# Twelve of each block's 32 scale and shift steps of a norm on VectorE in place of ScalarE

## The chip, the cores and the metric

The kernel runs on one core of one Trainium2 chip. The metric is the device time of one execution in microseconds. The weights lie in HBM; the two token blocks' activations stay in the core's memory from the first layer to the last.

## The reference

Two layers of a decoder over 256 tokens of width 2048. Each layer has a mixer and a SwiGLU FFN, each behind an RMS norm whose result is scaled and shifted per channel by vectors that are computed from a conditioning vector `c`:

```python
def rms_norm(x, gain):
    xf = x.astype(jnp.float32)
    y = xf * lax.rsqrt(jnp.mean(xf * xf, axis=-1, keepdims=True) + EPS)
    return (y * gain.astype(jnp.float32)).astype(x.dtype)
...
# a layer, in words:
#   shift1, scale1, gate1, shift2, scale2, gate2 = silu(c) @ w_mod + b_mod
#   x += gate1 * mixer(rms_norm(x) * (1 + scale1) + shift1) @ w_out
#   x += gate2 * (silu(h @ w_gate) * (h @ w_up)) @ w_down,  h = rms_norm(x) * (1 + scale2) + shift2
```

The mixer is one input projection `w_in`, whose columns go to gated linear attention (GLA), sliding-window attention and a gated DeltaNet, and one output projection `w_out`. Behind the last layer stands one more norm with `final_gain`, without scale and shift steps.

## The kernel before

The 256 tokens are two blocks of 128 (`NB`), the 2048 channels 16 tiles of 128 (`KD`). All large products go through `stream`: a weight's row of 128 channels comes by DMA into `raw` (L321, on SP's queue), ScalarE rounds it to `wh` (L328), VectorE makes the rest `wl = raw - wh` (L329), and TensorE multiplies both blocks' activations, themselves split in two parts `hm`, with them (L356). Rows that are taken whole (`k in whole`) skip L328 and L329; so does all of layer 0's `w_out`.

`norm(l, sub, blk, r, res)` makes the activations of one block; `sub` is 0 for the mixer's norm and 1 for the FFN's. It goes by groups `j` of four channel tiles. VectorE scales the block's 512 columns by the inverse root mean square `r` (L450), TensorE transposes the four tiles into one PSUM bank `ps` (L453; tag `ga` or `mm`, three banks in all), ScalarE applies scale and shift to each tile, from PSUM into the tile `h32` (L456, four steps), ScalarE rounds all four to `hm` (L459), and VectorE makes the rest (L460). Scale and shift are per-partition columns `mod_col`, since the channels are the partitions here. A block has four groups, so 16 steps, and a norm of both blocks 32. There are four norms between products: layer 0's mixer norm at the start, layer 0's FFN norm (566 to 585 us in the profile), layer 1's mixer norm (1365 to 1388) and layer 1's FFN norm (1817 to 1836).

The modulation vectors of later norms are computed in the background: `mod_segment` loads rows of `w_mod` into `mraw` (L218, SP) and VectorE multiplies and adds them into `acc` (L221, one 128x1024 instruction for a row). `rate` sets how many of these steps stand beside a weight row. In an FFN norm `held` puts a small column of the last group's `hm` into `hold`: the next `mraw` is first written by GpSimd from it (L216), so its load waits for the norm. Behind layer 1's FFN norm SP also loads `final_gain`, 1 MB, into `fg` (L1136).

At the end of the mixer the last group of input columns (264 + 264, for GLA) is evicted by ScalarE in pieces (L975), partly with SiLU, while the attention's softmax takes exponentials on ScalarE (L913, L916; its rows are `b`, `neg`, `tot`). SiLU and exponential need different function tables; an `ACT_TABLE_LOAD` stands where the set changes.

The order of the work is not that of the source. The framework's scheduler puts the instructions of each engine into one list by its own estimate of when each can start, and every engine works its list strictly in order; waits are put in where an operand comes from another engine, or a buffer or a PSUM bank is still in use there.

Of the kernel before, what the change touches and what calls it, by code (L numbers as in the profile page):

```python
# [15 lines left out]
AF = mybir.ActivationFunctionType  # L16
ALU = mybir.AluOpType
AX = mybir.AxisListType

P = 128  # L20
# [83 lines left out]
def trunk(ctx: ExitStack, tc, x, cT, pos, small, consts, b_mod, w_mod, w_in, w_gk, w_out,  # L104
# [22 lines left out]
    def tl(pool, shape, tag, dt=F32, bufs=None):  # L127
        return pool.tile(shape, dt, tag=tag, name=nm(tag), bufs=bufs)
# [5 lines left out]
    def bank(tag="mm"):  # L134
        if tag == "any":
            which[0] += 1
            tag = "ga" if which[0] % 3 == 0 else "mm"
        return tl(psm, [P, 512], tag, bufs=1 if tag == "ga" else 2)

    V, A, G, TE, SY = nc.vector, nc.scalar, nc.gpsimd, nc.tensor, nc.sync  # L140
# [55 lines left out]
    mod_col, gate_row = {}, {}  # L196
# [85 lines left out]
    def need(table, key):  # L282
        while key not in table:
            if fins:
                fins.popleft()[1]()
            else:
                mods.popleft()[1]()
        return table[key]
# [147 lines left out]
    def norm(l, sub, blk, r, res, ks=range(KD)):  # L436

        at = ks[0]
        while at <= ks[-1]:
            j, i0 = divmod(at, 4)  # L440
            n = min(4 - i0, ks[-1] + 1 - at)
            if j not in res:
                res[j] = (tl_h32(), *(tl(hmp, [P, 4, P], "hm", F32R) for _ in range(2)))
            h32, hh, hl = (t[:, i0:i0 + n] for t in res[j])
            xn = scr[0]()[:, :n * P]
            x_j = xs[:, blk, at * P:(at + n) * P]
            if XN_ACT[l][sub]:
                A.activation(xn, x_j, AF.Copy, scale=r)
            else:
                V.tensor_scalar(xn, x_j, r, None, ALU.mult)  # L450
            ps = bank("any")
            for i in range(n):
                TE.transpose(ps[:, i * P:(i + 1) * P], xn[:, i * P:(i + 1) * P], ident)  # L453
            for i in range(n):
                need(mod_col, (l, 3 * sub + 1, at + i))
                A.activation(h32[:, i], ps[:, i * P:(i + 1) * P], AF.Identity,  # L456
                             scale=mod_col[l, 3 * sub + 1, at + i],
                             bias=mod_col[l, 3 * sub, at + i])
            A.activation(hh, h32, AF.Copy)  # L459
            V.tensor_tensor(hl, h32, hh.bitcast(F32), ALU.subtract)  # L460
            at += n
        return res

    def tl_h32():
        return scr[0]().rearrange("p (a b) -> p a b", a=4)
# [491 lines left out]
    def layer(l):  # L957
# [94 lines left out]
        for bi, ks in enumerate(blocks):  # L1052
            first, last = bi == 0, bi == len(blocks) - 1
            rate[1] = RATE_LAST if last and l == 0 else RATE_IN[l]
            if last:
                closed.difference_update({(l, GATE1), (l, SHIFT2), (l, SCALE2)})
            for blk in range(NB):
                norm(l, 0, blk, rms[blk], h[blk], ks)
            for name in ("qk", "z", "v"):
                project(name)  # L1060
            if l == 0 and first:
                for o in range(0, n_mask, 512):
                    n = min(512, n_mask - o)
                    t = scr[1]()
                    SY.dma_start(t[:, :n], consts[:, N_FULL + o:N_FULL + o + n])
                    V.tensor_copy(masks[:, o:o + n], t[:, :n])
            if last:
                mix.clear()
                for blk in range(NB):
                    for group in (3, 1, 2):  # L1070
                        mix[blk, group] = tl(hmp, [P, 4, P], "hm")
                        G.memset(mix[blk, group][:, 0, 0:1], 0.0)
                    for name in ("gqk", "gv", "gz"):
                        G.memset(slot(hmp, "hm", (name, blk))[:, 0:1], 0.0)
                kT = swa_keys(pb, both("kv"))
                gdn(l, pg, [dict(enumerate(both(n))) for n in "qkv"], both("z"), both("cbca"))
            project("bq")
# [31 lines left out]
        def after_w_out(blk, j, ps, half, final):  # L1109
            add_gated(l, GATE1, blk, half * 2 + j, ps, final)  # L1110
            if final and half == 1 and j == 1:
                rms[blk] = inv_rms(blk)
                h[blk] = held(blk, norm(l, 1, blk, rms[blk], {}))
# [112 lines left out]
```

## Time and profile before

| | us |
|---|---|
| three runs | 2586.03, 2591.96, 2594.05 |
| their median | 2591.96 |
| the profiled execution | 2591.34 |
| its span | 2589.6 |
| TensorE busy | 2436.7 (94%) |
| VectorE busy | 1752.0 (68%) |
| ScalarE busy | 1067.0 (41%) |
| moved by DMA | 600.79 MB, 232 GB/s |

The span is the stretch from the first to the last instruction of the profiled execution; 1.7 us of the execution's time lie around it. Busy time counts instructions as the profiler saw them; an engine at 41% may still be the one that is waited for in one stage. PE is TensorE, DVE VectorE, ACT ScalarE, POOL GpSimd and SP the engine that issues the DMAs. The mean granted TensorE clock of the execution was 0.986 of 2.4 GHz.

### The profile page before, as it was taken

Reading aid. Unit: us, or ns where it says so; the run is one execution under the profiler, and the core shown is the slowest. Engines: PE = TensorE matmul, PEld = TensorE weight load, DVE = VectorE, ACT = ScalarE, POOL = GpSimd, SP = SyncE. Lnnn points to the kernel's source line nnn. Section 1 sums busy time; section 2 is a strip of 40 time slices with the busy share of each in tenths; the row PEclk is TensorE's granted clock in tenths of the full one; section 3 lists DMA queues with packets and bytes.
Section 4 is the critical chain, followed back from the end, with each engine's and each line's share of the span. In section 5 each row is a group of like instructions: output and inputs, shape, how many; then the busy total and the mean of one; then the engine's idle time right before and its main releaser. Section 6 shows DMA issues by size and latency. Waiting matters only on the chain.

```text
span 2589.6 us, 31057 instructions
## 1 busy us (share of the span) xinstructions
PE 2436.7 (94%) x11164; PEld 1885.3 (73%) x11164; DVE 1752.0 (68%) x2527; ACT 1067.0 (41%) x1582; POOL 26.4 (1%) x72
## 2 busy tenths in 40 slices
PE   4999999889999999999999999999899999999997
PEld 2555785447788777788767788877688878888876
DVE  7767876777666777657578788688664575544555
ACT  2203454134444333443445464654544434344443
POOL 0000000000000000000000000000000000000000
PEclk9999999999999999999999999999999999999999
DMA  9986548768778888868687875365676676566654
GB/s 336 367 314 215 179 141 274 270 198 283 261 258 277 280 277 278 279 192 297 217 282 233 283 227 157 96 197 187 213 251 194 204 275 194 188 193 188 188 179 155
DMA packets 190035, 600.79 MB, mean 232 GB/s; under 512 B 21628, under 2 KB 26268, under 8 KB 189496
## 3 DMA queue, kind: packets, MB, share of 16 engines
q1 hardware_dynamic: 189880, 598.81, 70.3%
q8 instruction: 87, 1.43, 0.2%
q14 instruction: 68, 0.56, 0.1%
HBM read 596.63 MB, written 2.10 MB: 231 GB/s over the span
## 4 chain that ended last, share of the span: by engine, by line
PE 54%; DMA 22%; DVE 13%; issue 8%; ACT 3%; SPq 0%; DVEq 0%; POOL 0%; ACTq 0%; POOLq 0%
PE acc L356 47%; DMA mraw<-in_w_mod 12%; DVE wl L329 4%; DVE acc L221 3%; DMA raw<-in_w_down 3%; DMA raw<-in_w_in 2%; DMA raw<-in_w_up 2%; DMA raw<-in_w_gate 2%; ACT wh L328 1%; PE mm L401 1%; PE ga L401 1%; PE ga L901 1%; PE mm L688 1%; DVE g L221 1%; PE ga L924 1%
## 5 line engine op out<-in xcount | busy, mean ns | idle before, releaser
L356 PE MATMUL acc<-wh,hm 128*128 128x512 f32 (+3 forms) x4872 | 1344.2, 389 | 19.7 <-ACT wh L328 6.2
L328 ACT ACTIVATE wh<-raw 128x1024 fp32r<-128x1024 f32 (+3 forms) x669 | 684.4, 1026 | 1022.5 <-PE acc L356 598.2
L329 DVE TENSOR_TENSOR wl<-raw,wh 128x1024 fp32r<-128x1024 f32 (+3 forms) x669 | 785.1, 1179 | 447.1 <-ACT wh L328 445.5
L356 PEld LDWEIGHTS acc<-wh,hm 128*128 128x128 f32 x4872 | 895.0, 189 | 215.5 <-issue 20.0
L356 PE MATMUL acc<-wl,hm 128*128 128x512 f32 (+3 forms) x2484 | 796.9, 395 | 9.0 <-DVE wl L329 6.7
L221 DVE SCALAR_TENSOR_TENSOR acc<-mraw,c_act,acc 128x1024 f32<-128x1024 f32 x320 | 410.3, 1282 | 225.3 <-DMA mraw<-in_w_mod 222.7
L356 PEld LDWEIGHTS acc<-wl,hm 128*128 128x128 f32 x2484 | 458.3, 190 | 119.2 <-DVE wl L329 18.0
L356 PE MATMUL acc<-wh,ahl 128*128 128x512 f32 x560 | 158.9, 397 | 0.2 <-ACT wh L328 0.2
L356 PEld LDWEIGHTS acc<-wh,ahl 128*128 128x128 f32 x560 | 106.1, 190 | 25.1 <-ACT wh L328 0.6
L221 DVE SCALAR_TENSOR_TENSOR g<-g,c_act,g 128x512 f32<-128x512 f32 x128 | 89.0, 746 | 11.2 <-DMA g<-in_w_mod 11.1
L356 PE MATMUL acc<-wl,ahl 128*128 128x512 f32 x280 | 91.3, 400 | 4.8 <-DVE wl L329 4.7
L356 PE MATMUL acc<-wh,b 128*128 128x512 f32 (+2 forms) x184 | 73.8, 540 | 3.3 <-ACT b L456 2.1
L356 PE MATMUL acc<-wl,b 128*128 128x512 f32 (+2 forms) x176 | 66.1, 513 | 1.8 <-DVE g L977 1.8
L356 PEld LDWEIGHTS acc<-wl,ahl 128*128 128x128 f32 x280 | 52.3, 189 | 20.7 <-DVE wl L329 9.2
L356 PE MATMUL acc<-raw,b 128*128 128x512 f32 (+2 forms) x176 | 66.8, 518 | 0.0
L356 PEld LDWEIGHTS acc<-wh,b 128*128 128x128 f32 x184 | 34.7, 195 | 32.6 <-issue 23.7
L456 ACT ACTIVATE b<-mm,mod,mod 128x128 f32<-128x128 f32 x24 | 9.2, 461 | 111.0 <-DVE mod L254 93.5
L356 PEld LDWEIGHTS acc<-wl,b 128*128 128x128 f32 x176 | 32.6, 190 | 29.0 <-issue 21.6
L356 PEld LDWEIGHTS acc<-raw,b 128*128 128x128 f32 x176 | 32.6, 190 | 26.6 <-issue 22.6
L937 DVE TENSOR_TENSOR acc<-acc,gate 128x512 f32<-128x512 f32 x64 | 42.9, 692 | 9.9 <-PE acc L356 9.2
L356 PE MATMUL acc<-raw,hm 128*128 128x512 f32 x88 | 42.9, 611 | 2.9 <-ACT acc L425 2.9
L939 DVE TENSOR_TENSOR xs<-xs,acc 128x512 f32<-128x512 f32 x64 | 42.3, 679 | 0.0
(329 smaller groups left out, 1663.6 us busy)
## 6 DMA issues: line engine op xcount, KB each, us to landing
mraw<-in_w_mod SPq DMA_DIRECT2D x320, 512.0 KB
raw<-in_w_down SPq DMA_DIRECT2D x176, 512.0 KB
raw<-in_w_gate SPq DMA_DIRECT2D x160, 512.0 KB
raw<-in_w_up SPq DMA_DIRECT2D x160, 512.0 KB
raw<-in_w_in SPq DMA_DIRECT2D x72, 512.0 KB
g<-in_w_mod SPq DMA_DIRECT2D x128, 256.0 KB
raw<-in_w_out SPq DMA_DIRECT2D x43, 512.0 KB
raw<-in_w_in SPq DMA_DIRECT2D x32, 264.0 KB
```

The source lines that it names most:

```text
L221: V.scalar_tensor_tensor(acc, raw[:, a], c_act[:, i + a:i + a + 1], acc, ALU.mult, ALU.add)
L328: A.activation(wh[:, :width], raw[:, :width], AF.Copy)
L329: V.tensor_tensor(wl[:, :width], raw[:, :width], wh[:, :width].bitcast(F32), ALU.subtract)
L356: TE.matmul(ps[blk, j][:, :segs[j][2]], xa, parts[j][part], start=i == 0 and n == 0, stop=last and n == len(terms) - 1)
L401: TE.transpose(ps[:, j * P:(j + 1) * P], src[:, j * P:(j + 1) * P], ident)
L456: A.activation(h32[:, i], ps[:, i * P:(i + 1) * P], AF.Identity, scale=mod_col[l, 3 * sub + 1, at + i], bias=mod_col[l, 3 * sub, at + i])
L688: TE.matmul(ps[:, s], LT[blk][:, s], Tm[blk][:, s], start=True, stop=True)
L901: TE.matmul(ps[:, j * nk:(j + 1) * nk], qT[rows, i + j], kT[rows, g, :nk], start=True, stop=True)
L924: TE.matmul(ps[:, j * 64:(j + 1) * 64], pT[:, j * nk + kb * P:j * nk + (kb + 1) * P], kv[kb][:, P + g * 64:P + (g + 1) * 64], start=kb == ...
L937: V.tensor_tensor(ps, ps, need(gate_row, (l, part, j)), ALU.mult)
L939: V.tensor_tensor(x_j, x_j, ps, ALU.add)
```

## The change

For every norm but the first of layer 0 (`l or sub`), the step of tile 1 of every group, and that of tile 3 in odd groups, is done by VectorE as one `tensor_scalar` with two per-partition columns (times scale, plus shift), from the same PSUM bank into the same tile `h32`. That is 6 of a block's 16 steps, 12 of a norm's 32, and 36 in the three norms.

```diff
@@ -453,9 +453,12 @@
                 TE.transpose(ps[:, i * P:(i + 1) * P], xn[:, i * P:(i + 1) * P], ident)
             for i in range(n):
                 need(mod_col, (l, 3 * sub + 1, at + i))
-                A.activation(h32[:, i], ps[:, i * P:(i + 1) * P], AF.Identity,
-                             scale=mod_col[l, 3 * sub + 1, at + i],
-                             bias=mod_col[l, 3 * sub, at + i])
+                scale, shift = (mod_col[l, 3 * sub + p, at + i] for p in (1, 0))
+                src = ps[:, i * P:(i + 1) * P]
+                if (l or sub) and (i == 1 or i == 3 and j % 2):
+                    V.tensor_scalar(h32[:, i], src, scale, shift, ALU.mult, ALU.add)
+                else:
+                    A.activation(h32[:, i], src, AF.Identity, scale=scale, bias=shift)
             A.activation(hh, h32, AF.Copy)
             V.tensor_tensor(hl, h32, hh.bitcast(F32), ALU.subtract)
             at += n
```

In the changed kernel VectorE's step is L459, ScalarE's L461, the rounding L462 and the subtraction L463; every line behind them is 3 higher than before (L913 is L916, L916 is L919, L975 is L978, L1136 is L1139). The scheduler makes other lists for all engines but GpSimd. Three places:

**VectorE in layer 1's mixer norm.** `g_9799`, `g_9815`, `g_9831`, `g_9847` are the tiles `h32` (and, as outputs of L450, `g_9818` and so on are the scaled columns `xn`) of successive groups; `acc_11744` is a modulation vector in the making. Before:

```order
L450 TENSOR_SCALAR g_9818<-xs_93,rms_2140_9774 128x512
L409 TENSOR_SCALAR rms_2143_9788<-rms_2143_9788 128x1 [waits DVE_49]
L410 TENSOR_SCALAR ss_2142_9785<-ss_2142_9785 128x1
L221 SCALAR_TENSOR_TENSOR acc_11744<-mraw_11747,c_act_100,acc_11744 128x1024 [waits DMAHW5_49,DMAHW3_49,Pool_49]
L413 TENSOR_SCALAR rs_2144_9789<-rms_2143_9788,ss_2142_9785 128x1 [waits DVE_49]
L450 TENSOR_SCALAR g_9834<-xs_93,rms_2140_9774 128x512
L417 SCALAR_TENSOR_TENSOR rms_2143_9788<-rs_2144_9789,rms_2143_9788 128x1 [waits DVE_49]
L460 TENSOR_TENSOR hm_9801<-g_9799,hm_9800 128x512 [waits Activation_49]
```

After:

```order
L459 TENSOR_SCALAR g_9799<-ga_9804,mod_0_8_1690_7451,mod_0_8_1541_6641 128x128 [waits Activation_49]
...
L221 SCALAR_TENSOR_TENSOR acc_11744<-mraw_11747,c_act_100,acc_11744 128x1024 [waits DMAHW5_49,DMAHW3_49,Pool_49]
...
L459 TENSOR_SCALAR g_9815<-mm_9820,mod_0_8_1690_7451,mod_0_8_1541_6641 128x128 [waits Activation_49]
...
L463 TENSOR_TENSOR hm_9801<-g_9799,hm_9800 128x512 [waits Activation_49]
...
L459 TENSOR_SCALAR g_9815<-mm_9820,mod_0_8_1690_7451,mod_0_8_1541_6641 128x128 [waits Activation_49]
...
L450 TENSOR_SCALAR g_9834<-xs_93,rms_2140_9774 128x512
...
L221 SCALAR_TENSOR_TENSOR acc_11744<-mraw_11786,c_act_100,acc_11744 128x1024 [waits DMAHW0_49]
L463 TENSOR_TENSOR hm_9817<-g_9815,hm_9816 128x512 [waits Activation_49]
L459 TENSOR_SCALAR g_9831<-mm_9836,mod_8_8_2030_9173,mod_8_8_1863_8305 128x128 [waits Activation_49]
L450 TENSOR_SCALAR g_9850<-xs_93,rms_2140_9774 128x512
...
L221 SCALAR_TENSOR_TENSOR acc_11744<-mraw_11822,c_act_100,acc_11744 128x1024 [waits DMAHW5_49,DVE_49]
L463 TENSOR_TENSOR hm_9833<-g_9831,hm_9832 128x512 [waits DVE_49,Activation_49]
```

The new steps (L459) wait for ScalarE, two of the four shown follow a modulation step (L221) with one row between, as does the next one, of `g_9847`, and the scaling of the third group, `g_9834`, has moved behind the first group's subtraction and the second group's two steps (rows of the inverse root, L408 to L417, and a row of the modulation vector are left out of the second list).

**ScalarE at the end of layer 0's FFN norm.** `s_4172` and `s_4188` are the tiles `h32` of the last two groups; `wh_4276` is the fourth row of the FFN's weights. Before:

```order
L456 ACTIVATE s_4172<-ga_4177,mod_8_8_973_3883,mod_8_8_1023_4073 128x128 x3
L456 ACTIVATE s_4188<-mm_4193,mod_8_8_973_3883,mod_8_8_1023_4073 128x128 [waits DVE_49,PE_49]
L459 ACTIVATE hm_4173<-s_4172 128x512 [waits Activation_49]
L456 ACTIVATE s_4188<-mm_4193,mod_8_8_973_3883,mod_8_8_1023_4073 128x128 x3
L328 ACTIVATE wh_4276<-raw_4274 128x1024 [waits DMAHW7_49]
L459 ACTIVATE hm_4189<-s_4188 128x512 [waits Activation_49]
L328 ACTIVATE wh_4297<-raw_4295 128x1024 [waits DMAHW1_49,PE_49]
L328 ACTIVATE wh_4318<-raw_4316 128x1024 [waits DMAHW2_49,PE_49]
```

After:

```order
L461 ACTIVATE s_4172<-ga_4177,mod_8_8_973_3883,mod_8_8_1023_4073 128x128 [waits DVE_49]
L461 ACTIVATE s_4172<-ga_4177,mod_8_8_973_3883,mod_8_8_1023_4073 128x128
L328 ACTIVATE wh_4276<-raw_4274 128x1024 [waits DMAHW7_49,PE_49]
L462 ACTIVATE hm_4173<-s_4172 128x512 [waits Activation_49]
L461 ACTIVATE s_4188<-mm_4193,mod_8_8_973_3883,mod_8_8_1023_4073 128x128 [waits PE_49]
L328 ACTIVATE wh_4297<-raw_4295 128x1024 [waits DMAHW1_49,PE_49]
L328 ACTIVATE wh_4318<-raw_4316 128x1024 [waits DMAHW2_49,PE_49]
L461 ACTIVATE s_4188<-mm_4193,mod_8_8_973_3883,mod_8_8_1023_4073 128x128 [waits DVE_49]
L462 ACTIVATE hm_4189<-s_4188 128x512 [waits DVE_49]
```

The rounding of the fourth weight row now stands ahead of the rounding `hm_4173` and of the last group's steps, the next two roundings stand between that group's steps, and ScalarE's steps of a group wait for VectorE's between them. In layer 1's FFN norm the rows have the same form.

**ScalarE at the end of layer 1's mixer.** `hm_10963`, `hm_10975` and `lr` are the evicted pieces of the last input product. ScalarE before:

```order
L920 ACTIVATE b_12439<-ga_12440 128x512 [waits PE_49]
L328 ACTIVATE wh_13581<-raw_13579 128x1024 [waits DMAHW3_49,PE_49]
L975 ACT_TABLE_LOAD
L975 ACTIVATE hm_10963<-acc_12890 128x264 [waits PE_49]
L975 ACTIVATE hm_10963<-acc_12891 128x248 [waits PE_49]
...
L975 ACTIVATE hm_10975<-acc_12898 128x264 [waits PE_49,Pool_49]
...
L328 ACTIVATE wh_13602<-raw_13600 128x1024 [waits DMAHW4_49]
L913 ACT_TABLE_LOAD
L913 ACTIVATE b_12455,tot_2743_12462<-b_12455,neg_2742_12460 128x256 [waits DVE_49]
```

ScalarE after:

```order
L328 ACTIVATE wh_13581<-raw_13579 128x1024 [waits DMAHW3_49,PE_49]
L978 ACT_TABLE_LOAD
L978 ACTIVATE hm_10963<-acc_12890 128x264 [waits PE_49]
L916 ACT_TABLE_LOAD
L916 ACTIVATE b_12425,tot_2735_12432<-b_12425,neg_2734_12430 128x256 [waits DVE_49]
...
L978 ACT_TABLE_LOAD
L978 ACTIVATE hm_10963<-acc_12891 128x248 [waits PE_49]
L919 ACT_TABLE_LOAD
L919 ACTIVATE neg_2734_12430<-neg_2734_12430 128x2 [waits DVE_49]
...
L978 ACTIVATE lr_2900_13222<-acc_12891 128x16
L978 ACT_TABLE_LOAD
L978 ACTIVATE hm_10975<-acc_12898 128x264 [waits Pool_49]
```

The exponentials of the attention (L916, L919) have moved in between the evictions (L978), each change with a table load: five of six are in these rows, and the last stands behind the remaining evictions, three rounded weights and a gate.

On SP's queue behind layer 1's FFN norm, `fg`, the load of `final_gain`, stood ahead of the loads of three w_gate rows (`raw_14568`, `raw_14586`, `raw_14604`) and now stands right behind them; the modulation's load ahead of it has moved behind eight more of w_gate.

## Rows read from the trace of the kernel before

**Rows 1.** The page: busy time of each engine (us, share of the span, instructions), and the chain of work that ended last, by engine.

```profile
PE 2436.7 (94%) x11164; PEld 1885.3 (73%) x11164; DVE 1752.0 (68%) x2527; ACT 1067.0 (41%) x1582; POOL 26.4 (1%) x72
...
PE 54%; DMA 22%; DVE 13%; issue 8%; ACT 3%; SPq 0%; DVEq 0%; POOL 0%; ACTq 0%; POOLq 0%
```

**Rows 2.** The windows view, nine stretches: from and to, length, then busy us and instructions of TensorE, its weight loads, VectorE, ScalarE and GpSimd, the granted TensorE clock (1.00 is 2.4 GHz, 0.50 is 1.2 GHz), the mean busy share of the DMA engines, and GB/s. The first three are the three norms, in the order of the program.

```profile
566.00:585.00 19.00, 15.84 (x70) 12.15 (x71) 10.04 (x27) 16.94 (x43) 0.00 (x0) 0.82 0.11 43
1365.00:1388.00 23.00, 19.64 (x84) 14.91 (x83) 20.43 (x37) 19.04 (x43) 1.51 (x13) 0.78 0.57 162
1817.00:1836.00 19.00, 15.48 (x73) 11.78 (x73) 10.80 (x28) 17.89 (x45) 0.72 (x1) 0.91 0.10 36
590.00:610.00 20.00, 18.18 (x78) 13.75 (x76) 14.51 (x12) 6.36 (x6) 0.00 (x0) 1.00 0.89 301
1410.00:1450.00 40.00, 36.34 (x242) 32.39 (x241) 29.70 (x33) 17.05 (x28) 0.00 (x0) 1.00 0.88 289
1683.00:1690.00 7.00, 7.00 (x38) 5.71 (x38) 4.52 (x8) 6.60 (x15) 0.00 (x0) 1.00 0.56 183
1665.00:1710.00 45.00, 43.80 (x271) 36.83 (x269) 31.28 (x56) 30.44 (x57) 0.95 (x1) 1.00 0.64 194
1840.00:1845.00 5.00, 3.51 (x16) 2.58 (x14) 0.00 (x0) 1.04 (x1) 0.00 (x0) 1.00 1.00 391
1845.00:1850.00 5.00, 4.88 (x13) 3.56 (x14) 4.90 (x5) 2.17 (x4) 0.00 (x0) 0.67 0.62 194
```

**Rows 3.** The timeline at the end of layer 0's FFN norm: start, us, engine, line, operation, out<-in, count [idle before <- what ended it].

```profile
581.88 0.69 ACT L459 ACTIVATE hm<-s 128x512 fp32r<-128x512 f32 x1
...
582.40 1.21 ACT L456 ACTIVATE s<-mm,mod,mod 128x128 f32<-128x128 f32 x3
...
583.43 1.13 ACT L328 ACTIVATE wh<-raw 128x1024 fp32r<-128x1024 f32 x1
...
584.61 1.20 PE L356 MATMUL acc<-wh,hm 128*128 128x512 f32 x4 [0.95 <-ACT wh L328]
```

**Rows 4.** Groups of instructions by line and form, whole span: busy us, mean ns of one, idle time before them and what ended it.

```profile
L221 DVE SCALAR_TENSOR_TENSOR acc<-mraw,c_act,acc 128x1024 f32<-128x1024 f32 x320 | 410.3, 1282 | 225.3 <-DMA mraw<-in_w_mod 222.7 <-DVE hm L336 0.3 <-DVE wl L329 0.2
...
L524 DVE SCALAR_TENSOR_TENSOR a<-ga,grs,hm 128x128 f32<-128x128 f32 x16 | 4.5, 344 | 0.1
...
L637 DVE TENSOR_SCALAR g<-consts,p 128x128 f32<-128x128 f32 x16 | 3.5, 278 | 0.0
```

**Rows 5.** The timeline of ScalarE behind layer 0's FFN norm.

```profile
591.75 1.06 ACT L328 ACTIVATE wh<-raw 128x1024 fp32r<-128x1024 f32 x1 [4.78 <-DMA raw<-in_w_gate]
...
599.54 1.06 ACT L328 ACTIVATE wh<-raw 128x1024 fp32r<-128x1024 f32 x1 [5.50 <-DMA raw<-in_w_gate]
...
605.36 1.06 ACT L328 ACTIVATE wh<-raw 128x1024 fp32r<-128x1024 f32 x1 [3.50 <-DMA raw<-in_w_gate]
```

**Rows 6.** The timeline of VectorE at the start of layer 1's mixer norm.

```profile
1366.72 1.27 DVE L221 SCALAR_TENSOR_TENSOR acc<-mraw,c_act,acc 128x1024 f32<-128x1024 f32 x1
...
1368.10 0.47 DVE L450 TENSOR_SCALAR g<-xs,rms 128x512 f32<-128x512 f32 x1
...
1368.90 0.69 DVE L460 TENSOR_TENSOR hm<-g,hm 128x512 fp32r<-128x512 f32 x1 [0.26 <-ACT hm L459]
```

**Rows 7.** The timeline of ScalarE at the end of layer 1's mixer, where the last input product is evicted.

```profile
1682.45 1.06 ACT L328 ACTIVATE wh<-raw 128x1024 fp32r<-128x1024 f32 x1 [0.21 <-PE acc L356]
1683.53 1.28 ACT L975 ACT_TABLE_LOAD   x1
1684.82 0.66 ACT L975 ACTIVATE hm<-acc 128x264 f32<-128x264 f32 x2
...
1687.61 1.28 ACT L913 ACT_TABLE_LOAD   x1
```

**Rows 8.** The same place in layer 0, ScalarE: the first and the last of six table loads (the others start at 397.39, 399.80, 401.49 and 403.56).

```profile
393.62 1.28 ACT L975 ACT_TABLE_LOAD   x1
...
405.61 1.28 ACT L913 ACT_TABLE_LOAD   x1
```

**Rows 9.** TensorE at that place in layer 0.

```profile
399.29 1.10 PE L356 MATMUL acc<-wl,hm 128*128 128x512 f32 x2 [1.25 <-ACT b L913]
...
402.99 1.12 PE L356 MATMUL acc<-wh,hm 128*128 128x512 f32 x2 [0.55 <-DMA wh<-in_w_out]
```

**Rows 10.** The DMA queue of SP behind layer 1's FFN norm, from its timeline.

```profile
1836.53 0.33 SPq L1136 DMA_DIRECT2D fg<-in_final_gain  x1
1836.90 2.23 SPq L321 DMA_DIRECT2D raw<-in_w_gate  x3
```

**Rows 11.** The waits of SP: what waited, what for, us in total, times, longest.

```profile
SPq L1136 <- DVE hm L460: 21.8, 1, 21.8
```

**Rows 12.** The timeline of ScalarE around the end of layer 1's FFN norm.

```profile
1833.48 1.17 ACT L328 ACTIVATE wh<-raw 128x1024 fp32r<-128x1024 f32 x1
...
1843.96 1.06 ACT L328 ACTIVATE wh<-raw 128x1024 fp32r<-128x1024 f32 x1 [6.91 <-DMA raw<-in_w_gate]
```

**Rows 13.** TensorE there.

```profile
1834.70 1.20 PE L356 MATMUL acc<-wh,hm 128*128 128x512 f32 x4 [0.98 <-ACT wh L328]
...
1845.07 1.21 PE L356 MATMUL acc<-wh,hm 128*128 128x512 f32 x4 [1.56 <-ACT wh L328]
```

## Prediction

> **What bounds the kernel now.** I read the busy shares and the chain of waits first. TensorE is busy for 94% of the span and holds 54% of the chain that ended last; ScalarE holds 3% of it [rows 1]. Taking work from ScalarE can therefore pay only where TensorE stands still for ScalarE, and that has to be found stage by stage. So the second view is the windows [rows 2]. I call the FFN norm of layer 0 N2 (566 to 585), the mixer norm of layer 1 N3 (1365 to 1388), and the FFN norm of layer 1 N4 (1817 to 1836). TensorE is busy 15.84 of 19, 19.64 of 23 and 15.48 of 19 us there, ScalarE 16.94, 19.04 and 17.89. All three norms together leave TensorE 10.0 us of idle time, so this is the order of size of what can be had. In N3 there is something else to see: VectorE is busy for 20.43 of the 23 us.
>
> The profiled execution took 2591.34 us, 0.6 below the median of the runs shown (2591.96). The sum is made against 2591.34. What a measurement of this kernel can tell from no change is about 0.3%, 7.8 us.
>
> **The change, part by part.** 36 steps of 128x128 leave ScalarE, 12 in each norm, and 36 VectorE steps are added. Near the end of N2 three scaling steps start at 582.40 and the next instruction follows at 583.43, so one step takes 0.343 us; a rounding follows its predecessor's start by 0.52 (581.88 to 582.40) [rows 3]. The 36 steps are 12.3 us of ScalarE, 4.1 in a norm. The price of the new VectorE step is not in the trace. The nearest rows are a TENSOR_SCALAR of 128x128 at 278 ns and, reading PSUM as the new one does, a SCALAR_TENSOR_TENSOR of 128x128 at 344 ns [rows 4]. I take 0.33, near the one that reads PSUM; it adds 4.0 us to VectorE in each norm.
>
> *Inside a group.* In the new order each VectorE step waits for ScalarE's step before it, and ScalarE's next waits for VectorE; all four read one PSUM bank and write one tile. A chain of four steps was 4 x 0.343 = 1.37 us and becomes 1.35 with two of them on VectorE (1.24 to 1.37 with 0.278 and 0.344): nothing worth counting is gained in a group by itself. A gain needs ScalarE to do another bank's work meanwhile; its bound is all 12.3. The Trainium skill, "PSUM — Partial Sum Buffer", section "PSUM bank collisions raise a hardware error", says that two engines must not touch one bank in the same partitions at once, reads included, and that the compiler puts a dependency between them. By that rule the gain inside a group is 0, without it up to 12.3 over the 24 groups of the three norms; no run here shows a collision, but the waits in the new order agree with the rule.
>
> *N2.* TensorE waits 0.95 us at 584.61 for the fourth FFN weight's rounding, which stands behind the last group's steps on ScalarE (583.43) [rows 3]. In the new order it is ahead of the previous group's rounding and of the last group's four steps, 0.52 + 1.37 = 1.89 earlier, less one hand-off of 0.33: 1.56, which covers the 0.95. So −0.95. The two roundings that now stand inside the last group's steps delay its tile by 2.1 us; it is first needed by the thirteenth weight row, nine rows later, which covers that. Behind N2 the stage is held by transfers: ScalarE waits 4.78, 5.50 and 3.50 for w_gate rows [rows 5], and the DMA share is 0.89 from 590 to 610 [rows 2]. Part is given back there; I take **−0.8**, bounds −4.1 (all that ScalarE sheds) and 0.
>
> *N3.* VectorE also runs the modulation steps of layer 1 here, at 1.28 us each [rows 4]. Its 20.43 us and 4.0 more are 24.4 in 23.0: it becomes the engine that is short, by 1.4 us. The order says the same. Six of the twelve new steps follow a 1.28 us step with at most a short row or a subtraction between. The third group's scaling by the norm, at 1368.10 before, now stands behind the first group's subtraction (which began at 1368.90 and takes 0.69) and a new step of 0.33 [rows 6]: 1369.9, 1.8 later, less a step that the subtraction comes earlier (0.34), 1.5. Late next is TensorE's transposition of that group, then its products. The mixer behind has room: TensorE is busy 36.34 of 40 us from 1410 to 1450, at a DMA share of 0.88 [rows 2], so it can swallow anything from nothing to all. I take **+1.2**; bounds −4.1 (ScalarE's shed work alone) and +7.7 (six steps each a full 1.28 late).
>
> *Activation tables at the end of layer 1's mixer.* The new lines don't stand here, but the order moves here too. Before, ScalarE evicts the six pieces of the last input product in one run after one table load, from 1684.82, and one more load follows at 1687.61; a load takes 1.28 [rows 7]. In the new order the attention's exponentials stand between the pieces, with six loads. Four more are 5.1 us on ScalarE, which rounds w_out's weights in the same stretch. From 1683 to 1690 TensorE is busy 7.00 of 7 us and ScalarE 6.60 [rows 2]. That leaves 0.4 to hide a load in, and I grant as much behind: 5.1 − 0.8 = **+4.3**. The lower bound is layer 0, which before has just this interleave, six loads from 393.62 to 405.61 [rows 8]: TensorE loses 1.25 + 0.55 = 1.8 us [rows 9]. Layer 1 is nearer to the upper end, since there ScalarE has weights to round and layer 0's w_out comes by transfer. Bounds +1.8 and +5.1.
>
> *N4.* The rounding moves as in N2, and TensorE's wait for it is 0.98 [rows 13], ScalarE's rounding being at 1833.48 [rows 12]: −1.0. The second part is on SP's queue. Before, the load of final_gain (1 MB) is issued at 1836.53, after SP stood 21.8 us for the norm [rows 11], and three w_gate loads follow at 1836.90 [rows 10]. ScalarE then waits 6.91 us for them [rows 12] and TensorE 1.56 at 1845.07 [rows 13], with the DMA engines full (1.00 at 391 GB/s from 1840 to 1845) [rows 2]. Now the three w_gate loads go ahead of it, so half a megabyte each comes sooner; the megabyte is then ahead of the next loads. Of the 1.56 I count 1.2. Behind that standstill the granted clock is 0.67 from 1845 to 1850, a mixture of the two levels, where it was 1.00 (2.4 GHz) in the window before [rows 2]; if it stays up, another 4.88 x 0.33 = 1.6 us come off, which I leave to the bound, since a transfer is still short there. Together **−2.2**; bounds −7.3 (4.1 + 1.56 + 1.6) and 0.
>
> The same number of DMAs is issued, and the rest of what the order moves lies where TensorE has weights at hand; I cost it at nothing, and where that cover is gone it is inside the bounds of N3.
>
> Sum: −0.8 + 1.2 + 4.3 − 2.2 = +2.5, 2591.3 + 2.5 = **2593.8 us**.
>
> **The rivals.**
> *ScalarE's shed work is TensorE's gain.* If hand-offs run beside other groups' work, 12.3 us come off: 2579.0. For it: ScalarE is busier than TensorE in N2 and N4 [rows 2]. Against it: one bank, one tile, a chain as long as before; and only 10.0 us of TensorE idle time exist there. 0.13.
>
> *Slower: N3's hand-offs stand behind modulation steps.* Then each of the six costs TensorE a full 1.28, 7.7 in place of 1.2: 2600.3. It decides where the transposes' PSUM banks are still held when TensorE wants the next one, which is when VectorE is over a step late. For it: VectorE's 20.43 of 23 us. Against: TensorE has products of earlier groups to do. 0.16.
>
> *The loads are hidden.* From 1665 to 1710 ScalarE is busy for 30.44 of 45 us [rows 2]; with 14.6 us of idle time about, the four loads can cost nothing: 2593.8 − 4.3 = 2589.5. Against it: TensorE's 43.80 of these 45 us leaves it no slack to catch up in. 0.12.
>
> *A table switch costs more than its load.* The rows speak against it: the rounding before the load ends at 1682.45 + 1.06 = 1683.51, the load starts at 1683.53 and the next instruction at 1684.82 [rows 7], 1.29 later. If each of four loads also had to wait for a rounding in flight (1.06), that is 4.2 more: 2598.0. 0.03. The Trainium skill, "ScalarE: Activation LUTs", section "What ACT_TABLE_LOAD costs", gives a switch about 1283 ns of load and a drain of about 1380 ns, 2.66 us in all; by it the four loads would be 10.6 us and the time about 2599.3. The load agrees with the trace; no drain is seen in these rows.
>
> **How the numbers follow.** The forecast itself has 0.56. Its terms miss by up to 3.3, 5.3, 2.5 and 5.1 us downward and 0.8, 6.5, 0.8 and 2.2 upward; as independent errors these are 8.4 and 7.0, so its own range is 2585 to 2601. With the spread of the three runs (5.9 below their median, 2.1 above) they become 10.3 and 7.3. I give **2583.5 to 2602**: the slow rival is inside, the fast one (0.13) is out. Faster by over 0.3% (below 2584.2) is the first rival, 0.13. Slower by over 0.3% (above 2599.7) is the second, 0.16. The rest is 0.71.
>
> **What would show it.** In the profile after: the new steps at 0.28 to 0.35 us, alternating with ScalarE's; N2's and N4's TensorE wait for the fourth weight gone; VectorE at 22 us or more of N3's 23; six table loads between 1680 and 1700 where two stood, and TensorE idle for 2 to 5 us in that stretch, on waits that ScalarE ends. Wrong would be: TensorE's waits in the three norms shrunk by 8 us or more, which is the first rival; N3 longer by over 5 us, which is the second; TensorE at 43 us or more of the 45 from 1665 on, which makes the loads free.

## The result

| | before | changed |
|---|---|---|
| median of ten runs, us | 2589.99 | 2601.78 |
| lowest and highest | 2586.03 to 2595.01 | 2591.32 to 2618.73 |
| the profiled execution and its span | 2591.34, 2589.6 | 2604.89, 2603.1 |
| its mean granted clock | 0.986 | 0.981 |

The ratio is 1.0047, with a 95% interval of 1.0027 to 1.0067: slower by 11.8 us, beyond the 0.3% that was named as the limit. The forecast was 2593.8 us and no change that can be told; the range ended at 2602.0 and just holds the time, but the direction does not stand. (The lower end of the interval, 1.0027, lies a little under that limit, and well clear of no change. The title's count is off: it is six of a block's 16 steps, twelve of a norm's 32, as the section on the change says.)

The page after, answering to [rows 1]. TensorE is busy for 9.1 us more, with the same 11,164 matmuls; a matmul at half clock is counted as busy for longer (four of L904 take 1.13 us at 1684.77, at a granted clock of 1.00, and 2.07 us at 1699.66, at 0.50).

```profile
PE 2445.8 (94%) x11164; PEld 1893.7 (73%) x11164; DVE 1763.0 (68%) x2563; ACT 1062.2 (41%) x1550; POOL 26.6 (1%) x72
...
PE 56%; DMA 22%; DVE 13%; issue 5%; ACT 3%; SPq 1%; DVEq 0%; ACTq 0%; POOL 0%; POOLq 0%
```

The windows of the three norms, answering to [rows 2] (the same lengths of time from the same point of each norm), and four windows at the end of layer 1's mixer. The columns are those of [rows 2].

```profile
565.00:584.00 19.00, 16.49 (x73) 12.74 (x74) 14.49 (x39) 13.72 (x30) 0.00 (x0) 0.82 0.05 17
1362.50:1385.50 23.00, 17.28 (x78) 13.29 (x76) 21.09 (x44) 14.26 (x29) 1.50 (x13) 0.85 0.47 137
1827.00:1846.00 19.00, 16.22 (x72) 12.87 (x73) 14.09 (x39) 13.95 (x31) 0.00 (x0) 0.82 0.01 6
1690.00:1695.00 5.00, 2.52 (x10) 1.45 (x10) 0.66 (x3) 4.92 (x9) 0.00 (x0) 1.00 0.72 239
1695.00:1700.00 5.00, 3.62 (x12) 2.88 (x13) 1.99 (x5) 4.83 (x10) 0.00 (x0) 0.58 0.36 107
1700.00:1705.00 5.00, 5.00 (x12) 3.49 (x12) 3.18 (x4) 0.37 (x1) 0.00 (x0) 0.50 0.42 120
1705.00:1710.00 5.00, 5.00 (x22) 4.02 (x21) 3.80 (x5) 3.20 (x4) 0.00 (x0) 0.89 0.63 190
```

ScalarE is busy for 13.72, 14.26 and 13.95 us in the norms where it was 16.94, 19.04 and 17.89. ScalarE has been relieved, and the kernel is slower. In the last four windows TensorE is busy for 2.52 of 5 us and then gets a clock of 0.58, 0.50 and 0.89; before, it was busy for all of 1683 to 1690 at 1.00 [rows 2].

To place the time I counted TensorE's matmuls in each trace and took the time between the starts of the same two of them, by their numbers. The columns: the stretch in the time of the kernel before; the numbers of its first and last matmul; what it takes in traces of kernels that do not touch what it depends on (mean, range, and how many: two traces of the kernel before, the rest of experiments); what it takes in two traces of the change; and the difference of the means.

| stretch | matmuls | untouched, us | changed, us | difference |
|---|---|---|---|---|
| 550 to 590, layer 0's FFN norm | 2054 to 2178 | 39.9 (39.8 to 40.3, 6) | 38.8, 38.6 | −1.2 |
| 590 to 660, behind it | 2178 to 2466 | 69.4 (68.7 to 70.1, 6) | 72.8, 73.2 | +3.6 |
| 1340 to 1470, layer 1's mixer norm and behind | 5346 to 5952 | 129.2 (127.3 to 130.8, 8) | 129.2, 132.8 | +1.8 |
| 1675 to 1805, end of layer 1's mixer | 7193 to 7831 | 130.6 (128.3 to 131.4, 9) | 134.8, 135.2 | +4.4 |
| 1820 to 1860, layer 1's FFN norm | 7877 to 8029 | 38.2 (36.5 to 40.3, 6) | 35.9, 35.9 | −2.2 |
| 1860 to 1950, behind it | 8029 to 8425 | 91.8 (89.7 to 93.8, 6) | 97.5, 94.9 | +4.4 |

The six differences, before rounding, sum to +10.7 of the 11.8. Stretches with many transfers wander by 2 to 4 us from trace to trace, so single ones of a microsecond are not more than an indication; the +1.8 of the third row is one of these. The two traces of e12 (below) are not among the untouched; with them the third and fourth rows would read +2.1 and +4.7. Equal numbers are equal work in each row (the same output columns in all), but for the fourth, where the new list has 224,104 columns for 225,048.

### The profile page after: what moved, and what is told of

Same layout as the page of the kernel before. It is cut to its first block, busy times and chain, and to the rows that moved or that the text cites. A ratio compares the mean times of both kernels' runs of the same rounds, so it can differ in the third digit from the quotient of the medians.

```text
span 2603.1 us, 31055 instructions
## 1 busy us (share of the span) xinstructions
PE 2445.8 (94%) x11164; PEld 1893.7 (73%) x11164; DVE 1763.0 (68%) x2563; ACT 1062.2 (41%) x1550; POOL 26.6 (1%) x72
## 4 chain that ended last, share of the span: by engine, by line
PE 56%; DMA 22%; DVE 13%; issue 5%; ACT 3%; SPq 1%; DVEq 0%; ACTq 0%; POOL 0%; POOLq 0%
PE acc L356 49%; DMA mraw<-in_w_mod 14%; DVE wl L329 4%; DVE acc L221 3%; DMA raw<-in_w_gate 2%; DMA raw<-in_w_down 2%; DMA raw<-in_w_up 2%; DMA raw<-in_w_in 2%; ACT wh L328 1%; PE mm L401 1%; PE ga L904 1%; PE ga L401 1%; PE mm L691 1%; PE mm L698 1%; PE ga L927 1%
## 5 line engine op out<-in xcount | busy, mean ns | idle before, releaser
L221 DVE SCALAR_TENSOR_TENSOR acc<-mraw,c_act,acc 128x1024 f32<-128x1024 f32 x320 | 410.4, 1283 | 223.2 <-DMA mraw<-in_w_mod 221.5
L221 DVE SCALAR_TENSOR_TENSOR g<-g,c_act,g 128x512 f32<-128x512 f32 x128 | 89.1, 747 | 11.8 <-DMA g<-in_w_mod 11.5
L356 PE MATMUL acc<-raw,b 128*128 128x512 f32 (+2 forms) x176 | 66.8, 518 | 0.8 <-DVE g L980 0.7
L461 ACT ACTIVATE b<-mm,mod,mod 128x128 f32<-128x128 f32 x24 | 9.2, 461 | 111.3 <-DVE mod L254 93.7
L940 DVE TENSOR_TENSOR acc<-acc,gate 128x512 f32<-128x512 f32 x64 | 43.1, 694 | 10.8 <-PE acc L356 10.7
```

Of the source, the lines that this page charges most:

```text
L221: V.scalar_tensor_tensor(acc, raw[:, a], c_act[:, i + a:i + a + 1], acc, ALU.mult, ALU.add)
L356: TE.matmul(ps[blk, j][:, :segs[j][2]], xa, parts[j][part], start=i == 0 and n == 0, stop=last and n == len(terms) - 1)
L461: A.activation(h32[:, i], src, AF.Identity, scale=scale, bias=shift)
L940: V.tensor_tensor(ps, ps, need(gate_row, (l, part, j)), ALU.mult)
```

## The experiments

Each was timed in turn with the kernel before on one chip; the ratio is to that. Changes of a per cent's fraction need the stretches of the table as much as the times.

**e1 to e4: parts of the change.** The condition `(l or sub) and (i == 1 or i == 3 and j % 2)` is replaced; O stands for its second half.

```diff
-                if (l or sub) and (i == 1 or i == 3 and j % 2):
+                if l and not sub and blk == 1 and j == 2 and i == 3:       # e1: one step
+                if sub and O or l and not sub and blk == 0 and O:          # e2: 30 steps
+                if (l and not sub) and O:                                  # e3: 12 steps
+                if (sub) and O:                                            # e4: 24 steps
```

Expected of e1: 

> Only one of the 36 steps is moved (layer 1's mixer norm, block 1, group 2, tile 3), but the scheduler makes the list with six table loads at the end of layer 1's mixer. Theory A (the new list of the rest of layer 1 costs the time, above all the four more table loads, and not the steps): slower by 7 to 13 us, +0.3 to +0.5%, with a delay of TensorE's work of about 10 us between 1683 and 1700 and a granted clock of 0.5 behind it. Theory B (the moved steps cost the time, by hand-offs that wait behind modulation steps): one step is 1.3 us at most, so within 0.1% of before.

Expected of e2: 

> 30 of the 36 steps are moved (all of both FFN norms, block 0 alone in layer 1's mixer norm); the list at the end of layer 1's mixer keeps its two table loads. Theory A: no slower than before; -1 to -5 us from the FFN norms and +0.5 from the mixer norm, -0.2 to 0%. Theory B: 30/36 of the 11.8 us that the change costs, about +10 us, +0.4%.

Expected of e3: 

> The 12 steps of layer 1's mixer norm alone; six table loads at the end of the mixer. Theory A: slower by 10 to 15 us, +0.4 to +0.6%, since the gains of the FFN norms are missing. Theory B: a third of the steps, about +4 us, or up to +8 if the waits behind modulation steps are all of it, which stand in this norm alone.

Expected of e4: 

> The 24 steps of both FFN norms; two table loads at the end of the mixer, and the load of final_gain behind three w_gate loads as in the change. Theory A: faster by 1 to 5 us, -0.2 to -0.05%. Theory B: two thirds of the steps, about +8 us, or nothing if only the waits behind modulation steps cost time.

Measured: e1 1.0023 (1.0010 to 1.0037), e2 1.0041 (1.0025 to 1.0058), e3 1.0027 (1.0009 to 1.0044), e4 1.0021 (1.0005 to 1.0037). One step, moved alone, costs half of the whole (it is tile 3 of an even group, which the change itself leaves on ScalarE, so it is not one of the 36; but TensorE's list from matmul 5952 to 7831 is there that of the change). For that half theory A is right, and B cannot be. But e2 and e4, with the old list at the end of the mixer, are slower too, which A said they would not be. Neither theory was the whole. The stretch 1675 to 1700 by itself takes 36.7 and 36.6 us in e1 and e3, as in the change (36.6), and 25.2 in e2 and e4; so the new list takes +11.4 there each time, of which 6.7 come back up to 1805. Part of both is only work that has moved: TensorE's matmuls 7193 to 7347 have 47,592 output columns in the new list and 42,520 in the old one, and those from 7347 to 7831 have 176,512 and 182,528.

**e5, e6: the FFN norms one by one, and each kernel traced a second time.** The conditions are `(l == 0 and sub) and O` and `(l and sub) and O`.

Expected of e5: 

> The 12 steps of layer 0's FFN norm alone. Theory F (a stage that starts earlier runs into transfers that are not earlier, and the new order of modulation and weight loads gives the early microsecond back twice over): slower by 2 to 4 us, the delay of TensorE's work -2 to -4 us at 600 and +1 to +3 at 625. Theory G (the FFN norms cost nothing and the 5 us of both together are the spread of the runs): within 1 us of before.

Expected of e6: 

> The 12 steps of layer 1's FFN norm alone, with the load of final_gain behind three w_gate loads. Theory F: between -1 and +3 us: 4 to 5 us faster at 1850, given back at 1915 to 1930, where VectorE stands at a modulation step whose row is late ahead of the first product of the gate. Theory G: -2 to -4 us, and no wait of more than 1 us at 1915 to 1930.

Expected of the kernel before, traced again: 

> The kernel before once more, for a second trace: how far the delay of TensorE's work wanders from stage to stage without any change. Theory A or F: the stages that differ in the change (575 to 625, 1680 to 1700, 1915 to 1930) stay within 2 us here; theory G: they wander as much as in the change.

Expected of the changed kernel, traced again: 

> The changed kernel once more, for a second trace. Theory A: again about 11 us between 1683 and 1700, with a granted clock of 0.5 behind. Theory F: again the wait of 3 to 5 us at about 1930 on VectorE's product, behind a modulation step.

Measured: e5 1.0016 (0.9999 to 1.0034), e6 1.0003 (0.9986 to 1.0019), so neither is told from no change by its time. Their stretches speak for theory F: in e5 590 to 660 takes 71.1 us (69.4 untouched), in e6 1820 to 1860 takes 34.7 (38.2) and 1860 to 1950 99.1 (91.8). The second trace of the kernel before stays within 0.7 us of the untouched mean in 550 to 590 and in 590 to 660; that of the change repeats 36.6 us from 1675 to 1700.

What happens behind layer 0's FFN norm is seen on GpSimd and SP. GpSimd's L216 is the copy from the last group's `hm` that releases the held modulation load (`hold`). Before:

```profile
566.98 1.50 ACT L456 ACTIVATE s<-ga,mod,mod 128x128 f32<-128x128 f32 x4 [0.89 <-PE ga L453]
```

```profile
585.14 0.72 POOL L216 COPY mraw<-hm 128x1 f32<-128x1 f32 x1 [25.03 <-ACT hm L459]
```

After:

```profile
565.88 0.46 ACT L461 ACTIVATE s<-ga,mod,mod 128x128 f32<-128x128 f32 x1 [0.83 <-PE ga L453]
```

```profile
586.07 1.05 POOL L216 COPY mraw<-hm 128x1 f32<-128x1 f32 x1 [27.09 <-ACT hm L462]
```

From the norm's first scaling step to the release it was 585.14 − 566.98 = 18.2 us and is 586.07 − 565.88 = 20.2 (17.8 and 20.1 in the second traces). SP after:

```profile
582.99 2.38 SPq L321 DMA_DIRECT2D raw<-in_w_gate  x2
587.14 0.81 SPq L218 DMA_DIRECT2D mraw<-in_w_mod  x2
588.06 1.19 SPq L321 DMA_DIRECT2D raw<-in_w_gate  x2
594.65 1.65 SPq L218 DMA_DIRECT2D mraw<-in_w_mod  x2
596.39 2.15 SPq L321 DMA_DIRECT2D raw<-in_w_gate  x2
600.64 3.05 SPq L218 DMA_DIRECT2D mraw<-in_w_mod  x2
```

SP before:

```profile
563.33 0.36 SPq L218 DMA_DIRECT2D mraw<-in_w_mod  x1
...
585.89 0.33 SPq L218 DMA_DIRECT2D mraw<-in_w_mod  x1
586.62 1.29 SPq L321 DMA_DIRECT2D raw<-in_w_gate  x2
```

In the kernel before one modulation load goes out at 563.33, 22 us ahead of the release, and the held one at 585.89, with two w_gate loads 0.7 us behind it. In the change two w_gate loads stand ahead of both in SP's list, go out at 582.99 and 585.04, and both modulation loads follow the release, at 587.14 and 587.53. So SP's list has changed behind layer 0's FFN norm too, which the section on the change does not list, and a row of 0.5 MB that was moved while the norm left the DMA engines all but idle (0.11, [rows 2]) now falls into the stretch that waits for transfers. By the DMA packets between the same matmuls the change moves 4.1 MB from 550 to 590, where the untouched kernels moved 4.5 to 4.8, and 21.6 and 21.7 MB from 590 to 660, where they moved 20.7 to 21.1; at its 297 GB/s the 0.7 MB more are an estimated 2.4 of the 3.6 us. TensorE then waits for w_gate rows up to 619; in the kernel before the last such wait ended at 601, and at 603 in its second trace ([rows 5] show ScalarE's side of it).

```profile
604.38 0.73 PE L356 MATMUL acc<-wh,hm 128*128 128x512 f32 x2 [0.87 <-ACT wh L328]
...
611.67 1.21 PE L356 MATMUL acc<-wh,hm 128*128 128x512 f32 x4 [0.74 <-ACT wh L328]
...
618.81 1.20 PE L356 MATMUL acc<-wh,hm 128*128 128x512 f32 x4 [1.05 <-ACT wh L328]
```

**e7 to e9: the hold a group earlier.**

```diff
-                hold[:] = [res[3][1][:, 0, 0:1].bitcast(F32)]
+                hold[:] = [res[2][1][:, 0, 0:1].bitcast(F32)]
```

e7 is e4 with it, e8 the kernel before with it, e9 the whole change with it.

Expected of e7: 

> The 24 steps of both FFN norms as before (e4), and the modulation loads behind them are held until the third group's rounding, not the last one's; SP's order of modulation and w_gate loads in layer 0 is then again that of the kernel before. Theory H (the last group's rounding comes 2 us later in the change, and the modulation loads, which are held for it, come later and fall on the weights): the stretch 590 to 660 takes 69.4 us as before and not 72.3, 550 to 590 keeps its -0.9; in layer 1, 1910 to 1950 falls from 44.2 to about 40.4 and 1820 to 1860 stays at 35.4; in all -3 to -5 us against before. Theory G (spread): as e4, +5 us.

Expected of e8: 

> The kernel before with the same early hold and no step moved. Theory H: 0 to -2 us, since a hold that comes a group earlier lets the modulation loads start 2 to 3 us earlier; it gives no 0.9 in 550 to 590. If the early hold itself were a gain of 5 us or more, e7 would say nothing on the steps.

Expected of e9: 

> The whole change with the early hold; six table loads at the end of layer 1's mixer remain. Theory H: 5 to 7 us less than the change, so +0.2 to +0.3% against before, made of +4.8 (the table loads' stretch, 1675 to 1805), about +1 (layer 1's mixer norm) and -1 to -3 in the FFN norms. Theory A alone (the list is all): as the change, +0.47%.

Measured: e7 0.9992 (0.9976 to 1.0008), e8 0.9983 (0.9967 to 0.9998), e9 1.0020 (1.0007 to 1.0032). The release in e7 comes 578.34 − 562.80 = 15.5 us behind the first step:

```profile
578.34 0.71 POOL L216 COPY mraw<-hm 128x1 f32<-128x1 f32 x1 [22.88 <-ACT hm L462]
```

590 to 660 takes 69.0 us in e7 and 68.9 in e9, as without the change, and 550 to 590 keeps its gain (38.4 and 38.7); e7's trace is that of the shortest of its twelve executions. The edit moves more than the release: SP's list behind layer 0's FFN norm is that of the kernel before again, and the modulation row goes out ahead of the release (at 558.75 in e7, 557.7 in e9), so these two runs do not tell the one from the other. 1860 to 1950 takes 94.8 and 93.8, where the change had 97.5 and 94.9 and the untouched kernels 91.8, so in layer 1 some 2 us of the 4.4 come back.

e9 is 0.27% below the change: the earlier hold is worth about 7 us of its 11.8, give or take 6 by the two intervals. Not all of this is a cost of the change, since e8 gains 4.4 us (0.5 to 8.5) by the same edit with no step moved, close to the 5 us at which, by the expectation, e7 would say nothing on the steps; in e8 590 to 660 takes 66.8 us, 2.1 less than in e7 and e9. e8 is the fastest of all versions run; e7, which moves 24 steps, is not faster than it. That the steps on VectorE are worth anything to the whole time is shown nowhere.

**e10: four table loads and no step moved.** In layer 1, behind each SiLU piece:

```diff
                     if first:
                         A.activation(dst, ps[:, lo:hi], func if last else AF.Copy)
+                        if last and func == AF.Silu and ...:
+                            t = tl(smp, [P, 1], "dummy")
+                            A.activation(t, dst[:, 0:1], AF.Exp)
```

Expected: 

> The kernel before, with four exponentials of one column put between the evictions of the last input product in layer 1, which makes six table loads out of two and moves no step of a norm. Theory A: 1675 to 1700 takes 8 to 12 us more than 25.2, with TensorE's clock at 0.5 behind; of that 6 to 7 are given back only if the order behind is that of the change, which it is not here, so +5 to +12 us in all. Rival (the loads are hidden, it is the other order that costs): under 2 us.

Measured: 0.9997 (0.9981 to 1.0013). 1675 to 1700 takes 30.8 us, 5.6 more, and 1675 to 1805 takes 134.7, 4.1 more than untouched; but the time does not show it. Its interval ends at +3.4 us, a little under that 4.1. TensorE's waits there:

```profile
1692.86 1.10 PE L924 MATMUL ga<-kv,b 128*128 128x64 f32 x8 [0.34 <-ACT b L920]
1694.46 0.66 PE L401 MATMUL ga<-consts,b 128*128 128x128 f32 x4 [0.49 <-DVE b L928]
1695.89 0.63 PE L757 MATMUL ga<-consts,hm 128*128 128x128 f32 x4 [0.78 <-ACT hm L503]
1697.39 0.80 PE L356 MATMUL acc<-wh,hm 128*128 128x512 f32 x1 [0.87 <-ACT lr L975]
```

They are spread, 2.5 us in all, and the clock falls for 3.4 us; in the change one wait of 3.25 stands among 4.5, and the clock is at half for 10.2 us. So four loads alone are not yet the 11.4 us; the other part of it lies in TensorE's own list, which is not that of the change here (41,752 columns up to matmul 7347 for its 47,592). Between the stretch, which agrees with the change's, and the time, which does not, this run leaves open what the loads alone are worth at the end.

**e11, e12: all 36 steps without the two costs, and one cost without a step.** e11 has the early hold and, in layer 1's mixer norm, tile 3 of the even groups for that of the odd (`j % 2 == 0`), which gives two table loads. e12 is the kernel before with a later hold:

```diff
-                hold[:] = [res[3][1][:, 0, 0:1].bitcast(F32)]
+                hold[:] = [res[3][2][:, 0, 0:1].bitcast(F32)]
```

Expected of e11: 

> 36 steps again, 12 in each of the three norms (in layer 1's mixer norm tile 3 of the even groups in place of the odd ones), with the early hold; the list at the end of layer 1's mixer has two table loads. If the late hold and the new list are the whole of the change's cost: as e7 or e8, -0.15 to +0.05% against before, 25.2 us from 1675 to 1700. If the steps themselves cost in the mixer norm (the rest of what e9 has over e7): as e9, +0.15 to +0.3%.

Expected of e12: 

> The kernel before with no step moved and the hold later: the modulation loads wait for the last group's subtraction, not its rounding, which ends about 1.4 us later. Theory H: +2 to +5 us, 590 to 660 at 71 to 73 us and 1910 to 1950 at 42 to 45. Rival (the weights' order or the steps cost the time in the FFN norms, not the hold): within 1 us of before.

Expected of e12, traced again: 

> The kernel before with the late hold once more, for a trace of another of its executions, since the traced one was its shortest by far (2579.8, the others' median 2595.6). Theory H: 590 to 660 at 71 to 73 us in an execution of about 2595. Rival: the time lies in stretches that have no hold.

Measured: e11 1.0012 (0.9993 to 1.0032); e12 1.0036 (1.0015 to 1.0056). e12 settles that a later hold slows this kernel with no step moved: 9 us (4 to 15), twice what was expected. It changes SP's list as well, so the late release and the order of the loads are not told apart here either: in layer 0 one w_gate load goes ahead of both modulation loads, in layer 1 the modulation load that stood ahead of `fg` goes out behind three w_gate loads. e11 is no longer told from no change, though it lies above what was expected; its trace has 135.3 us from 1340 to 1470, 6 more than untouched (e2: 133.8). It is not the other tiles alone, since e2 moves the change's own. Whether the mixer norm's steps cost time stays open: the other traces that move them have 128.3 (e3), 129.2 and 132.8 (the change) and 130.2 us (e9), and the three above 132 are those with some 20 us at half clock in this stretch, where the others have 3 to 14.

The stretch behind layer 0's FFN norm is not where e12's time lies (68.8 and 70.3 us, against the expectation), though the release is as late there as in the change (20.0 and 19.9 us behind the first step) and 21.8 MB are moved. So without the moved steps neither the late release nor the row that moved costs that stretch anything that these two traces show. Part of e12's time is in layer 1: 1910 to 1950 takes 42.8 and 44.0 us, against 40.3 untouched and 44.2 in the change and its parts (the mean of five traces, 41.2 to 45.9). The second trace:

```profile
1918.39 1.28 DVE L221 SCALAR_TENSOR_TENSOR acc<-mraw,c_act,acc 128x1024 f32<-128x1024 f32 x1 [2.12 <-DMA mraw<-in_w_mod]
1919.59 0.68 DVE L1146 TENSOR_TENSOR s<-s,acc 128x512 f32<-128x512 f32 x1
...
1920.33 0.66 PE L401 MATMUL mm<-consts,s 128*128 128x128 f32 x4 [3.50 <-DVE s L1146]
```

Before the first product of the gate (`s`, L1146) VectorE does a modulation step (L221) whose row comes 2.12 us late, and TensorE, which transposes the product, waits 3.50. In the change the same three instructions stand with longer waits:

```profile
1928.37 1.28 DVE L221 SCALAR_TENSOR_TENSOR acc<-mraw,c_act,acc 128x1024 f32<-128x1024 f32 x1 [3.28 <-DMA mraw<-in_w_mod]
1929.57 0.68 DVE L1149 TENSOR_TENSOR s<-s,acc 128x512 f32<-128x512 f32 x1
...
1930.31 1.12 PE L401 MATMUL mm<-consts,s 128*128 128x128 f32 x4 [4.66 <-DVE s L1149]
```

The rest of e12's 9 us was not placed.

## Why the prediction was wrong, point by point

**N2 and N4, the step that failed.** The prediction had "The two roundings that now stand inside the last group's steps delay its tile by 2.1 us; it is first needed by the thirteenth weight row, nine rows later, which covers that." The 2.1 us were right (2.0 and 2.4 in two traces, measured on the release in layer 0; 3.1 in layer 1), and so was the gain ahead of it, −0.95 forecast and −1.2 measured in layer 0, −2.2 and −2.2 in layer 1. But the tile has another reader. A modulation load is held for it, and the loads behind it on SP's queue stand in a stretch whose limit is the transfers. The cover that was named hid the products' need and not the loads'. A second sentence failed with it: "the rest of what the order moves lies where TensorE has weights at hand; I cost it at nothing". In both FFN norms the order moved a modulation load out of the norm's idle transfer time (in layer 0 from 563.33 to 587.14). These two made N2 +2.4 in place of −0.8, and N4 +2.1 in place of −2.2: 7.5 of the 9.3 us between the +2.5 forecast and the +11.8 measured. In N4 the order on SP, read as a gain of 1.2 alone, has its price at 1930, 80 us later, where the modulation rows that were moved back are missed; the change moves 24.6 and 24.7 MB from 1860 to 1950, the untouched kernels 23.5 to 23.9.

What e4 (1.0021), e7 (0.9992) and e8 (0.9983) show is that the moved steps of the FFN norms cost time with the hold where it was, and none that can be told with the hold a group earlier. Which part is the late release and which the order of the loads stays open, and e12 speaks against either being enough in layer 0 by itself.

**The tables.** Five of the six loads stand between 1688 and 1697, the sixth at 1708.54, and there is no drain:

```profile
1688.54 1.28 ACT L978 ACT_TABLE_LOAD   x1
1689.84 0.39 ACT L978 ACTIVATE hm<-acc 128x264 f32<-128x264 f32 x1
1690.25 1.28 ACT L916 ACT_TABLE_LOAD   x1
...
1692.65 1.28 ACT L978 ACT_TABLE_LOAD   x1
...
1694.34 1.28 ACT L919 ACT_TABLE_LOAD   x1
...
1695.75 0.58 ACT L923 ACTIVATE b<-ga 128x512 f32<-128x512 f32 x1
...
1696.42 1.28 ACT L978 ACT_TABLE_LOAD   x1
```

TensorE's waits there are 0.94, 0.26 and 3.25, together 4.5 us, where 2 to 5 were named:

```profile
1690.28 0.50 PE L356 MATMUL acc<-wh,hm 128*128 128x512 f32 x1 [0.94 <-ACT hm L978]
...
1692.20 0.93 PE L401 MATMUL ga<-consts,b 128*128 128x128 f32 x4 [0.26 <-ACT b L916]
1696.38 1.97 PE L927 MATMUL ga<-kv,b 128*128 128x64 f32 x8 [3.25 <-ACT b L923]
```

The stretch to 1805 costs 4.4 where 4.3 was forecast, but by another path than the sum's: 11.4 up to 1700, of which 4.5 are TensorE's waits and 5.1 the clock's (10.2 us at 1.2 GHz behind the windows in which TensorE was half idle), and 7.0 back up to 1805. Over the whole stretch TensorE's idle time is 12.6 and 12.8 us in the change and 11.8 in the mean of the nine untouched traces, only 0.9 more, where the sum had 4.3 of standing still; most of the rest is the clock, at half for 13.7 us where it was 7.6 on the mean (3.4 to 10.2). That the size agrees is luck. By the time e1 shows the new list to cost 6 us; what the four loads cost without it stays open (e10). The lower bound was misread, too: of layer 0's 1.8 us, 0.55 is a wait for a transfer [rows 9], which leaves 1.25. The load's 1.28 us agrees with what the Trainium skill states in "ScalarE: Activation LUTs", section "What ACT_TABLE_LOAD costs". The drain of 1.38 us that it adds to a switch is not in this trace: the instruction ahead of the load of 1690.25 ends 0.02 us before it, and after the load of 1688.54 the next activation starts 1.30 us after the load did.

**N3.** +1.2 forecast, +1.8 measured, from 129.2 and 132.8 us, inside or near the untouched 127.3 to 130.8, so neither the term nor its absence is shown. VectorE is busy for 21.09 of 23 us, under the 22 that were named as a sign. The rival of 7.7 us did not come in the change's two traces.

**The hand-offs.** A group in layer 0's FFN norm (`s<-mm`), with one VectorE step between ScalarE's; ScalarE fits in a step of the next bank (`s<-ga`) meanwhile:

```profile
575.11 0.46 ACT L461 ACTIVATE s<-mm,mod,mod 128x128 f32<-128x128 f32 x1 [0.92 <-PE mm L453]
...
575.47 0.45 ACT L461 ACTIVATE s<-ga,mod,mod 128x128 f32<-128x128 f32 x1
575.61 0.41 DVE L459 TENSOR_SCALAR s<-mm,mod,mod 128x128 f32<-128x128 f32 x1 [0.57 <-ACT s L461]
...
576.05 0.81 ACT L461 ACTIVATE s<-mm,mod,mod 128x128 f32<-128x128 f32 x2
...
576.75 0.63 ACT L462 ACTIVATE hm<-s 128x512 fp32r<-128x512 f32 x1
```

From the first step to the rounding it is 1.64 us, where four steps in a row on ScalarE are 4 × 0.343 = 1.37 by [rows 3]. VectorE's step is 0.41 us in the median of 36, outside the bounds taken (0.28 to 0.34), and a ScalarE step that follows nothing takes its whole 0.46 and not the 0.343 of steps that overlap. The rule on one bank for one engine at a time ("PSUM — Partial Sum Buffer", section "PSUM bank collisions raise a hardware error", in the Trainium skill) fits these rows, in which the two engines do not overlap on this group's bank; so would the wait on the shared tile.

**The rivals.** The fast one is out: ScalarE is 3 to 5 us less busy in each norm, and TensorE gains 1 to 2 in two of them at once. The slow one had the right sign with the wrong mechanism; that a held transfer could be late, or another be put behind it, stood among none of them. The range's upper end was generous as well: the prediction's own sum, 2593.8 + 7.3, ends at 2601.1, below the 2601.8 measured.

## What to carry to other kernels

When an edit delays a value, list all its readers, those that exist only to time something too, before calling the delay covered; a value that releases transfers can be worth what the stage of those transfers is short of. Relieving an engine that is busier than the bound can gain inside its stage, as 1.2 and 2.2 us here, and lose more in the stage behind it. Where a scheduler writes the lists, compare them for the whole program, the DMA queue's with them, and price each place apart: here one moved step of 0.41 us changed a list 300 us later, and the time by half of what 36 did.

## What was not expected of the hardware

A step of 128x128 from PSUM with two per-partition columns takes 0.41 us on VectorE, more than the two nearest rows said (278 and 344 ns). A stretch of 5 us in which TensorE was busy 2.52 was followed by 10.2 us at 1.2 GHz; in e10, with 2.5 us of idle time spread over 4.5, it was 3.4 us.
